# A head's query, gate and forget products in one row of groups, squares held back, and the last output weights loaded in another order

## The chip, the cores and the metric

The kernel runs on one core of one Trainium2 chip. The metric is the device time of one execution in microseconds (us). The kernel before takes 2017.0 us, the median of 3 runs (2017.0 to 2017.1).

## What is computed

The input is one sequence of 512 tokens of width 1024. A first block mixes tokens in two ways side by side, an HGRN2 recurrence with 4 heads of 128 and an NSA attention with 8 query heads of 64 in 2 groups, and adds a gated feed-forward step. Then come two layers of a second kind (L0 and L1), each with stick-breaking attention, differential attention and a feed-forward step of width 4096, and a last norm. All is in float32. The parts that the change touches are these:

```python
def hgrn2_mixer(hq, hf, hi, hg, lb, o_gain):
    q = jax.nn.silu(hq).reshape(B, T, H, dk)
    f = lb + (1.0 - lb) * jax.nn.sigmoid(hf)
    logf = jnp.log(f).reshape(B, T, H, dk)
    k = (1.0 - f).reshape(B, T, H, dk)
    ...
    o = rms_norm(o, o_gain) * jax.nn.silu(hg).reshape(B, T, H, dv)

def first_block(...):
    h = rms_norm(x, norm_mix[l])
    ...
    q = rms_norm(q.reshape(B, T, H, dh), q_norm[l])
    kc = rms_norm(compress(kc_raw, ...), k_norm[l, 0])
    vc = compress(vc_raw, ...)
    ...
    mix = jnp.concatenate([o_nsa, o_hgrn], axis=-1)
    x = x + mix @ w_out[l]

def differential_attention(q, k, v, lam):        # in L0 and L1
    ...
    p = jax.nn.softmax(jnp.where(allowed, s, neg), axis=-1)
    attn = p[:, :, 0] - lam * p[:, :, 1]
    return jnp.einsum('bhqk,bhkd->bhqd', attn, vh)
```

## The kernel before

Activations lie feature by token: a tile has 128 features on its partitions and all 512 tokens in its columns. A weight product ("group") takes a tile of 128 output features and goes over 8 tiles of input. `load_w` (L393 to L396) fetches a weight, ScalarE casts it into a high part (`_h`) and VectorE subtracts to get the low part (`_l`); `mm3` (L401, L402, L403) then does three matmuls for each input tile. There are two buffers for the parts and two PSUM banks of the kind "mm" for the results. `gemm_fm` runs such groups and calls an `emit` function on each finished bank; `gemm_nat` does the same with tokens on the partitions.

In the first block four streams of work (the HGRN heads, the set-up of NSA, its attention and the weight groups, `dense1`) are merged by `_drive`. A planner, `Clock`, keeps a rough time for each engine; a stream that would wait is passed over and the next one asked. The weight groups come in the order of a string, `ORDER1`: q1 is the query and forget product of head 1 (`whqf`), g0 is the output gate of head 0 (`whg`), n4 is the fifth NSA product (`wns`), i1 is the value product, v0 the NSA value and gate product (`wvsw`), w1 the second half of the output product (`wout1`); m4 waits for a head to be finished. The Tile scheduler then sets the final order on each engine.

The names that the steps below use:

- `emit_hgrn` (L607) and `emit_gate` (L627): scale a bank by the norm, take a sigmoid on ScalarE, multiply; for the forget product also a logarithm and a scan along the tokens. [...]
- `hgrn_head`: for each of the levels 64 to 1, decayed queries and keys (`qr`, `ke`) and 8 small matmuls `hpl` (L695), whose result VectorE selects into `at` (L697); then `hpd`, `hpo`, `hpv` (L754) and the head's output `ho`, transposed on TensorE (`ho_t`, L558).
- `emit_nsa` (L776): of each query product the parts `nq` and a square `nsq` (L789, ScalarE), and right behind it four matmuls `pq` (L792) that sum the square over a head's features. The groups after it follow in program order.
- `cs` (L927), `sc` (L930 to L948), `cpt` (L957): the scores of the compressed keys, their softmax on VectorE and ScalarE, and their transpose.
- the attention in 32 steps: scores `s` (L981 to L983), softmax `p`, transposes `pt` (L1014) and values `po`. The first matmul of a value (L1028) uses 32 rows and 64 columns of the array, the others (L1033) 128 rows and 64 columns.
- `gemm_late`: the other half of the output product, `wout0` (L0wo1 and L1wo1 in the layers). It starts when the attention has sent off its last scores, keeps four groups open until the last input exists, finishes them, and then runs the other four (`wout0x`, `L0wo1x`), whose weights come through the same two buffers.
- in L0 and L1 the scores `ds` (L1298 to L1301), transposes `dpt` (L1325) and values `dfo` (L1337) of the differential attention; `head_squares` (L532, `dsq`) reads the values' bank on ScalarE after each of its four steps. `L0wo` and `L1wo` are the output products, `add_residual` (L491) adds a bank to `X`.

## Time and profile before

| | before |
|---|---|
| median of 3 runs | 2017.0 us |
| profiled execution, its own time | 2017.01 us |
| span of that execution | 2015.1 us |
| TensorE busy | 1974.8 us, 98% of the span |
| VectorE busy | 1176.9 us, 58% |
| ScalarE busy | 885.1 us, 44% |
| mean granted clock of TensorE | 0.993 of full speed |

The span is what the profile covers; 1.9 us of the execution's own time lie around it. "Busy" is the share of the span in which an engine had an instruction running. The granted clock is given as a share of full speed, 1.00 for 2.4 GHz and 0.50 for 1.2 GHz.

### The profile page before, as it was taken

To read this page: it belongs to the slowest core of one execution; us is meant where nothing else is said; L and a number is where in the kernel's file an instruction comes from. 1 tells how busy PE (TensorE), PEld (TensorE's weight loads), DVE (VectorE), ACT (ScalarE), POOL (GpSimd) and SP (SyncE) were. 2 spreads that over 40 slices of the span, in tenths; PEclk is the share of its full clock that TensorE was granted. 3 is DMA by queue.
4 is the path that set the end of the run, shared out by engine and by line. 5 is a ranking of instruction groups with operands and counts; after the bars stand their busy time and mean duration, and the time that the engine had idled before them with its cause. 6 is when DMAs were issued, how large, how long until landed. Compare 5 with 4: busy or idle time off the path is not lost.

```text
span 2015.1 us, 25957 instructions
## 1 busy us (share of the span) xinstructions
PE 1974.8 (98%) x10197; PEld 1610.1 (80%) x10197; DVE 1176.9 (58%) x2032; ACT 885.1 (44%) x1497; POOL 45.2 (2%) x87
## 2 busy tenths in 40 slices
PE   8999999999999999999999999999999999999998
PEld 7888866788888878787778888888888778888887
DVE  7687676744444456557764444447466874444446
ACT  6645355522222235687542223335587743322223
POOL 1000000000000000001000000000000000000000
PEclk9999899999999999999999999999999999999999
DMA  6212100122222222212122222223221222222222
GB/s 206 67 60 88 51 22 22 53 95 96 99 97 95 95 89 92 82 40 84 61 84 98 100 95 94 94 94 105 79 64 58 63 76 98 98 94 94 95 94 74
DMA packets 50922, 168.65 MB, mean 84 GB/s; under 512 B 5808, under 2 KB 8240, under 8 KB 50800
## 3 DMA queue, kind: packets, MB, share of 16 engines
q1 hardware_dynamic: 47680, 161.93, 23.4%
q0 software_dynamic: 2976, 4.98, 1.2%
q8 instruction: 81, 1.33, 0.3%
q14 instruction: 41, 0.34, 0.1%
q10 hardware_dynamic: 144, 0.07, 0.0%
HBM read 160.14 MB, written 2.10 MB: 81 GB/s over the span
## 4 chain that ended last, share of the span: by engine, by line
PE 88%; DVE 5%; ACT 5%; issue 2%; DMA 1%; SPq 0%; DVEq 0%; POOL 0%; ACTq 0%
PE L0wf_p L403 6%; PE L0wf_p L401 6%; PE L0wf_p L402 6%; PE L1wf_p L403 5%; PE L1wf_p L401 5%; PE L1wf_p L402 5%; PE wgu_p L403 4%; PE wgu_p L401 4%; PE wgu_p L402 4%; PE wdn_p L401 2%; PE wdn_p L402 2%; PE wdn_p L403 2%; PE po L1033 1%; PE hpl L695 1%; PE pt L1014 1%
## 5 line engine op out<-in xcount | busy, mean ns | idle before, releaser
L395 ACT CAST L0wf_h<-L0wf_r 128x1024 fp32r<-128x1024 f32 x64 | 67.3, 1051 | 228.1 <-PE L0wf_p L403 224.8
L395 ACT CAST L1wf_h<-L1wf_r 128x1024 fp32r<-128x1024 f32 x60 | 63.1, 1051 | 219.7 <-PE L1wf_p L403 216.7
L403 PE MATMUL wgu_p<-h_l,wgu_h 128*128 128x512 f32 x328 | 128.8, 393 | 0.0
L401 PE MATMUL wgu_p<-h_h,wgu_h 128*128 128x512 f32 x328 | 128.7, 392 | 0.0
L402 PE MATMUL wgu_p<-h_h,wgu_l 128*128 128x512 f32 x328 | 128.6, 392 | 0.0
L395 ACT CAST wgu_h<-wgu_r 128x1024 fp32r<-128x1024 f32 x44 | 46.2, 1050 | 162.9 <-issue 62.8
L401 PE MATMUL L0wf_p<-L0u_h,L0wf_h 128*128 128x512 f32 x256 | 100.7, 393 | 0.0
L402 PE MATMUL L0wf_p<-L0u_h,L0wf_l 128*128 128x512 f32 x256 | 100.4, 392 | 0.0
L403 PE MATMUL L0wf_p<-L0u_l,L0wf_h 128*128 128x512 f32 x256 | 99.4, 393 | 0.0
L403 PE MATMUL L0wf_p<-L0m_l,L0wf_h 128*128 128x512 f32 x240 | 94.2, 393 | 0.0
L403 PE MATMUL L1wf_p<-L1m_l,L1wf_h 128*128 128x512 f32 x240 | 94.2, 393 | 0.0
L401 PE MATMUL L0wf_p<-L0m_h,L0wf_h 128*128 128x512 f32 x240 | 94.2, 392 | 0.0
L401 PE MATMUL L1wf_p<-L1m_h,L1wf_h 128*128 128x512 f32 x240 | 94.2, 392 | 0.0
L402 PE MATMUL L1wf_p<-L1m_h,L1wf_l 128*128 128x512 f32 x240 | 94.1, 392 | 0.0
L402 PE MATMUL L0wf_p<-L0m_h,L0wf_l 128*128 128x512 f32 x240 | 94.1, 392 | 0.0
L396 DVE TENSOR_TENSOR L0wf_l<-L0wf_r,L0wf_h 128x1024 fp32r<-128x1024 f32 x64 | 78.4, 1226 | 24.7 <-ACT L0wf_h L395 24.7
L401 PE MATMUL L1wf_p<-L1u_h,L1wf_h 128*128 128x512 f32 x224 | 88.1, 393 | 0.0
L402 PE MATMUL L1wf_p<-L1u_h,L1wf_l 128*128 128x512 f32 x224 | 87.9, 392 | 0.0
L396 DVE TENSOR_TENSOR L1wf_l<-L1wf_r,L1wf_h 128x1024 fp32r<-128x1024 f32 x60 | 73.5, 1225 | 23.2 <-ACT L1wf_h L395 23.2
L403 PE MATMUL L1wf_p<-L1u_l,L1wf_h 128*128 128x512 f32 x224 | 86.9, 393 | 0.0
L491 DVE TENSOR_TENSOR X<-X,L0wf_p 128x512 f32<-128x512 f32 x64 | 44.0, 687 | 67.1 <-PE L0wf_p L403 67.1
L491 DVE TENSOR_TENSOR X<-X,L1wf_p 128x512 f32<-128x512 f32 x56 | 38.6, 689 | 66.5 <-PE L1wf_p L403 66.5
(879 smaller groups left out, 5397.2 us busy)
## 6 DMA issues: line engine op xcount, KB each, us to landing
L0wf_r<-w_ff SPq DMA_DIRECT2D x64, 512.0 KB, 3.2
L1wf_r<-w_ff SPq DMA_DIRECT2D x60, 512.0 KB, 3.3
wgu_r<-w_gu SPq DMA_DIRECT2D x44, 512.0 KB, 3.2
wdn_r<-w_dn SPq DMA_DIRECT2D x22, 512.0 KB, 3.2
wns_r<-w_nsa SPq DMA_DIRECT2D x8, 512.0 KB, 3.5
L0wsb_r<-w_sbqk SPq DMA_DIRECT2D x8, 512.0 KB, 3.2
L0wdf_r<-w_dfqk SPq DMA_DIRECT2D x8, 512.0 KB, 3.2
L1wsb_r<-w_sbqk SPq DMA_DIRECT2D x8, 512.0 KB, 3.2
```

What stands on the lines that cost most here:

```text
L395: S.copy(hi[:, c], raw[:, c])
L396: V.tensor_tensor(lo[:, c], raw[:, c], _f(hi)[:, c], ALU.subtract)
L401: TE.matmul(ps, lh, rh, start=start, stop=False)
L402: TE.matmul(ps, ll, rh, start=False, stop=False)
L403: TE.matmul(ps, lh, rl, start=False, stop=stop)
L491: V.tensor_tensor(X[m], X[m], ps, ALU.add)
L695: TE.matmul(pl[:, b * 64 : (b + 1) * 64], ke[:, b * P : (b + 1) * P], qr[:, b * 64 : (b + 1) * 64], start=True, stop=True)
L1014: TE.transpose(pt[:, o + j * P : o + (j + 1) * P], p[g][:, j * P : (j + 1) * P], ident)
L1033: TE.matmul(po[g * 64 : (g + 1) * 64, 0:P], vsw[:, j, br * 128 + g * 64 : br * 128 + (g + 1) * 64], p[g][:, j * P : (j + 1) * P], start=Fa ...
```

## The change

`ORDER1` gets a new kind of entry. `x1` is the function `together`: it runs the query product of head 1, the output gate of head 0 and the forget product of head 1 in a row, without the sigmoids between them, and writes all sigmoids behind. `x2` does so for head 2 and gate 1, `x3` for head 3 and gate 2. The entries q1 to q3 and g0 to g2 are gone.

The sums of squares leave `emit_nsa`. A stream of its own, `nsa_squares`, sends off the four `pq` matmuls when the planner has the square done and a bank free; at the latest the next finished group does it (`catch_up`). `nsa_setup` waits for all six.

`gemm_late` loads its first two weights at its start and no longer waits for the last scores; its first two open groups use the "mm" banks, the other two the spare ones. Its third weight is loaded before the end, into buffers that are free by then ("kh", "kl").

The first value matmul of a step uses all 128 rows: `vz` holds the compressed values in four blocks of 128 columns, zero outside a block's own 32 rows. GpSimd makes it with a memset and four copies.

In the layers the planner has a value step wait until it believes that the last reader of the bank is done (`clock.read`).

```diff
-ORDER1 = "i0 q1 g0 n4 i1 q2 n6 g1 n0 m4 n7 n1 g2 m5 q3 n5 n2 n3 v0 g3 m7 w1"
+ORDER1 = "i0 x1 n4 i1 x2 n6 n0 m4 n7 n1 m5 x3 n5 n2 n3 v0 g3 m7 w1"

+    def read(self, tile):
+        self.take()
+        e, at = self.used.get(tile.tensor.name, ("PE", 0.0))
+        while e != "PE" and self.free["PE"] < at + 0.2:
+            yield None

-    def gemm_late(src, hs, emit, name, banks):
+    def gemm_late(src, hs, emit, name, scored, spare_banks):
         yield from until(lambda: all(x is not None for x in hs[:3]))
+        loaded = [load_w(src[b], f"{name}_{b}") for b in range(2)]
         for b in range(2):
-            wh, wl = load_w(src[b], f"{name}_{b}")
+            wh, wl = loaded[b]
+            if b == 1:
+                yield from until(scored)
+                loaded = [load_w(src[2], f"{name}_2", ("kh", "kl"))]
+                banks = spare_banks()
             for m in range(cols // P):
-                ps = banks.pop(0)() if banks else bank("mm", f"{name}_p{b}_{m}")
+                ps = bank("mm", f"{name}_p{b}_{m}") if b == 0 else banks[m]
...
-        yield from gemm_fm(src[2:], hs, emit, name + "x", 2 * (cols // P))
+        yield from gemm_fm(src[2:], hs, emit, name + "x", 2 * (cols // P), loaded=loaded)

+        def together(h, gates):
+            pre = []
+            def emit(m, ps):
+                catch_up()
+                x = sb("evt", f"x{h}_{len(pre)}")
+                V.tensor_tensor(x, ps, rb1, ALU.mult)
+                pre.append(x)
...
+            yield from gemm_fm(d["w_hqf"][2 * h : 2 * h + 1], h1, emit, f"whq{h}")
+            for g in gates:
+                yield from gemm_fm(d["w_hg"][g : g + 1], h1, emit, f"whg{g}")
+            yield from gemm_fm(d["w_hqf"][2 * h + 1 : 2 * h + 2], h1, emit, f"whf{h}")
+            x, hs_ = pre[-1], slice(h, h + 1)
+            forget = gated("kD", f"hk{h}", x)
+            q_ = gated("kC", f"hq{h}", pre[0])
+            gate = [gated("hs", f"hs{g}", pre[1 + i]) for i, g in enumerate(gates)]
+            with exp_ln_tables():
+                S.activation(x, forget, AF.Ln, scale=oml[:, hs_], bias=lbg[:, hs_])
...
+        def nsa_squares():
+            while len(squared) < 6:
+                yield from until(lambda: waiting or len(squared) == 6)
...
+                for w in (ready(sq), bank_free("t", 2)):
+                    for _ in w:
+                        if not waiting or waiting[0][0] != m:
+                            break
+                        yield None
+                if waiting and waiting[0][0] == m:
+                    add_squares()
+                    yield "low"

         def emit_nsa(m, ps):
+            catch_up()
...
             S.activation(sq, ps, AF.Square)
-            pq = bank("t", f"pq{m}")
-            for tb in range(NB):
-                TE.matmul(pq[:, 2 * tb : 2 * tb + 2], sq[:, tb * P : (tb + 1) * P], blk2, start=True, stop=True)
...
+            waiting.append((m, sq))

-                        TE.matmul(po[g * 64 : (g + 1) * 64, 0:P], comp["v"][32 * i : 32 * i + 32, g * 64 : (g + 1) * 64],
-                                  pct[g][32 * i : 32 * i + 32, qs], start=True, stop=False, tile_position=(32 * i, g * 64))
+                        TE.matmul(po[g * 64 : (g + 1) * 64, 0:P], vz[:, i * P + g * 64 : i * P + (g + 1) * 64],
+                                  pct[g][:, qs], start=True, stop=False)

-                     lambda n: both(ready(st[n], dv[NB - 1]), bank_free("o", 1) if n % NB == 0 else ()))))
+                     lambda n: both(ready(st[n], dv[NB - 1]), bank_free("o", 1) if n % NB == 0 else clock.read(st["do"])))))
```

The next pieces show TensorE's order at three places. Rows with x4 or x2 stand for as many instructions alike.

The first place is the levels of head 3, where the squares of the fourth query product (`nsq3`) are summed. Before:

```order
L695 MATMUL hpl3_8_1894<-qr3_8_1887,ke3_8_1888 128x64 x4
L403 MATMUL wvsw_p0_1982<-wvsw_1_l_1978,h1_6_h_145 128x280
L401 MATMUL wvsw_p0_1982<-wvsw_1_h_1977,h1_7_h_149 128x280
L402 MATMUL wvsw_p0_1982<-wvsw_1_h_1977,h1_7_l_150 128x280
L403 MATMUL wvsw_p0_1982<-wvsw_1_l_1978,h1_7_h_149 128x280
L792 MATMUL pq3_1951<-packed_82,nsq3_1949 128x2
L695 MATMUL hpl3_4_1932<-qr3_4_1913,ke3_4_1914 128x64 x4
L792 MATMUL pq3_1951<-packed_82,nsq3_1949 128x2 x3
L401 MATMUL wvsw_p1_2037<-wvsw_0_h_1971,h1_0_h_121 128x280
```

After:

```order
L411 MATMUL wvsw_p0_1941<-wvsw_1_l_1937,h1_6_h_145 128x280
L409 MATMUL wvsw_p0_1941<-wvsw_1_h_1936,h1_7_h_149 128x280
L410 MATMUL wvsw_p0_1941<-wvsw_1_h_1936,h1_7_l_150 128x280
L411 MATMUL wvsw_p0_1941<-wvsw_1_l_1937,h1_7_h_149 128x280
L747 MATMUL hpl3_4_2032<-qr3_4_1974,ke3_4_1975 128x64 x4
L409 MATMUL wvsw_p1_2005<-wvsw_0_h_1930,h1_0_h_121 128x280
L410 MATMUL wvsw_p1_2005<-wvsw_0_h_1930,h1_0_l_122 128x280
L411 MATMUL wvsw_p1_2005<-wvsw_0_l_1931,h1_0_h_121 128x280
L835 MATMUL pq3_1954<-packed_82,nsq3_1914 128x2 x4
L409 MATMUL wvsw_p1_2005<-wvsw_0_h_1930,h1_1_h_125 128x280
```

The four `pq3` were split by a level and followed the last of `wvsw_p0`; now they stand together, one level and three matmuls of `wvsw_p1` later, and the level `hpl3_8` stands 24 matmuls of `wvsw_p0` ahead of `hpl3_4`.

The second place is the start of the attention, around the transpose of the last head's output (`ho3_t`). Before, with the eight `cpt` matmuls in two rows right ahead of `s2_1`, that is four rows above this piece:

```order
L981 MATMUL s3_0_2428<-nk1h_2108,nq0_1175 128x256
L982 MATMUL s3_0_2428<-nk1l_2109,nq0_1175 128x256
L983 LDWEIGHTS masks_106
L983 MATMUL s3_0_2428<-masks_106 128x128
L981 MATMUL s3_1_2433<-nk1h_2108,nq0_1175 128x256
L982 MATMUL s3_1_2433<-nk1l_2109,nq0_1175 128x256
L983 LDWEIGHTS masks_106
L983 MATMUL s3_1_2433<-masks_106 128x128
L981 MATMUL s4_0_2462<-nk0h_2087,nq0_1175 128x384
L982 MATMUL s4_0_2462<-nk0l_2088,nq0_1175 128x384
L558 MATMUL ho3_t_2318<-packed_82,ho3_2303 128x128 x4
L1014 MATMUL pt0_0_2348<-packed_82,p0_2341 128x128 x2
```

After:

```order
L1061 MATMUL s3_0_2433<-nk1h_2114,nq0_1169 128x256
L1062 MATMUL s3_0_2433<-nk1l_2115,nq0_1169 128x256
L1063 LDWEIGHTS masks_106
L1063 MATMUL s3_0_2433<-masks_106 128x128
L572 MATMUL ho3_t_2296<-packed_82,ho3_2269 128x128 x4
L1094 MATMUL pt0_0_2332<-packed_82,p0_2325 128x128 x2
L1061 MATMUL s3_1_2438<-nk1h_2114,nq0_1169 128x256
L1062 MATMUL s3_1_2438<-nk1l_2115,nq0_1169 128x256
L1063 LDWEIGHTS masks_106
L1063 MATMUL s3_1_2438<-masks_106 128x128
L1037 MATMUL cpt0_2376<-packed_82,sc_2149 128x128 x3
L409 MATMUL wout1_p0_0_2342<-ho3_m_h_2301,wout1_0_h_2337 128x512
```

The transposes `cpt0` and `cpt1` moved from ahead of `ho3_t` to behind it, and the last score product `s4_0` ahead of it is gone. Further up, all twelve last matmuls of `whg3` stood behind the last `cs` before; they all stand ahead of it now.

The third place is the end of the differential attention in L0 (L1 is alike). Before:

```order
L402 MATMUL L0wo1_p1_0_8638<-L0do3_m_h_8625,L0wo1_1_l_8634 128x512
L403 MATMUL L0wo1_p1_0_8638<-L0do3_m_l_8626,L0wo1_1_h_8633 128x512
L401 MATMUL L0wo1_p1_1_8648<-L0do3_m_h_8625,L0wo1_1_h_8633 128x512
L401 MATMUL L0wl_8578<-L0do3_m_h_8625,L0wo1_0_h_8580 128x512
L402 MATMUL L0wl_8578<-L0do3_m_h_8625,L0wo1_0_l_8581 128x512
L403 MATMUL L0wl_8578<-L0do3_m_l_8626,L0wo1_0_h_8580 128x512
L402 MATMUL L0wo1_p1_1_8648<-L0do3_m_h_8625,L0wo1_1_l_8634 128x512
L403 MATMUL L0wo1_p1_1_8648<-L0do3_m_l_8626,L0wo1_1_h_8633 128x512
L401 MATMUL L0wo1x_p0_0_8680<-L0do0_m_h_7900,L0wo1x_0_h_8675 128x512
L401 MATMUL L0wo1x_p0_1_8694<-L0do0_m_h_7900,L0wo1x_0_h_8675 128x512
```

After:

```order
L409 MATMUL L0wo1_p0_0_8576<-L0do3_m_h_8642,L0wo1_0_h_8565 128x512
L410 MATMUL L0wo1_p0_0_8576<-L0do3_m_h_8642,L0wo1_0_l_8566 128x512
L409 MATMUL L0wo1_p0_1_8597<-L0do3_m_h_8642,L0wo1_0_h_8565 128x512
L410 MATMUL L0wo1_p0_1_8597<-L0do3_m_h_8642,L0wo1_0_l_8566 128x512
L411 MATMUL L0wo1_p0_0_8576<-L0do3_m_l_8643,L0wo1_0_h_8565 128x512
L411 MATMUL L0wo1_p0_1_8597<-L0do3_m_l_8643,L0wo1_0_h_8565 128x512
L409 MATMUL L0wl_8633<-L0do3_m_h_8642,L0wo1_1_h_8571 128x512
L410 MATMUL L0wl_8633<-L0do3_m_h_8642,L0wo1_1_l_8572 128x512
L411 MATMUL L0wl_8633<-L0do3_m_l_8643,L0wo1_1_h_8571 128x512
L409 MATMUL L0wo1x_p0_0_8677<-L0do0_m_h_7917,L0wo1_2kh_8628 128x512
```

The groups that were finished first were those of the spare bank (`L0wl`); now they are those of the "mm" banks, and the group behind them, `L0wo1x_p0_0`, reads the weight `L0wo1_2kh`, whose cast stands some twenty instructions further up on ScalarE than that of `L0wo1x_0_h` did.

## Rows read from the trace of the kernel before

**Rows 1.** The page: busy time, share of the span and instructions of each engine.

```profile
PE 1974.8 (98%) x10197; PEld 1610.1 (80%) x10197; DVE 1176.9 (58%) x2032; ACT 885.1 (44%) x1497; POOL 45.2 (2%) x87
```

**Rows 2.** TensorE's waits: line, what it waited for, us in total, times, longest.

```profile
PE pq L792 <- ACT nsq L789: 4.5, 4, 2.2
PE s L981 <- ACT p L993: 2.2, 2, 1.6
...
PE L0dfo L1337 <- ACT L0dsq L532: 1.2, 2, 0.9
...
PE L0wo1x_p L401 <- ACT L0wo1x_h L395: 0.8, 1, 0.8
...
PE cpt L957 <- DVE sc L948: 0.8, 1, 0.8
PE hpl L695 <- DVE ck_u L834: 0.7, 1, 0.7
...
PE L0wo1x_p L402 <- DVE L0wo1x_l L396: 0.6, 1, 0.6
...
PE wout0x_p L402 <- DVE wout0x_l L396: 0.6, 1, 0.6
PE pkc L853 <- DVE ck_u L837: 0.6, 1, 0.6
```

**Rows 3.** Windows: stretch, length, busy PE, PEld, DVE, ACT, POOL, PEclk, DMA share, GB/s.

```profile
200.76:204.17 3.41, 3.41 (x17) 3.41 (x16) 2.56 (x4) 1.85 (x3) 0.00 (x0) 0.50 0.33 126
...
207.59:214.40 6.81, 6.34 (x29) 6.35 (x30) 2.25 (x6) 0.83 (x2) 0.00 (x0) 0.50 0.01 1
214.40:221.24 6.84, 6.84 (x32) 6.84 (x32) 3.59 (x15) 0.35 (x1) 0.00 (x0) 0.50 0.01 2
...
1013.13:1016.55 3.42, 3.42 (x9) 2.65 (x8) 2.76 (x4) 2.34 (x5) 0.00 (x0) 0.50 0.75 220
```

**Rows 4.** Timeline of the levels of head 3: start, us, instruction, idle before.

```profile
196.68 1.00 PE L695 MATMUL hpl<-qr,ke 128*128 128x64 f32 x8
...
199.15 1.05 PE L792 MATMUL pq<-packed,nsq 128*128 128x2 f32 x8 [1.47 <-ACT nsq L789]
...
208.06 0.59 PE L792 MATMUL pq<-packed,nsq 128*128 128x2 f32 x2 [2.23 <-ACT nsq L789]
...
213.03 1.80 PE L695 MATMUL hpl<-qr,ke 128*128 128x64 f32 x8
```

**Rows 5.** Window from the last compressed score to `ho3_t`, columns as above.

```profile
240.08:256.63 16.55, 14.23 (x84) 11.53 (x84) 15.22 (x49) 10.71 (x27) 0.00 (x0) 1.00 0.09 32
```

**Rows 6.** Window of the matmuls of `whg3` alone: PE, PEld, DVE, PEclk.

```profile
240.08:242.77 2.69, 2.69 (x12) 1.99 (x11) 0.00 (x0) 1.00 0.00 0
```

**Rows 7.** Timeline from the last compressed score to the first values.

```profile
244.34 1.28 ACT L631 ACT_TABLE_LOAD   x1
245.63 0.63 ACT L631 ACTIVATE gsg<-gx 128x512 f32<-128x512 f32 x1
...
252.31 1.09 PE L957 MATMUL cpt<-packed,sc 128*128 128x128 f32 x8 [0.76 <-DVE sc L948]
...
255.52 0.69 DVE L551 TENSOR_TENSOR ho<-hpv,ho_rn 128x512 f32<-128x512 f32 x1
255.63 0.38 PE L981 MATMUL s<-nk1h,nq 128*128 128x256 f32 x1 [1.56 <-ACT p L993]
...
261.80 0.43 PE L1028 MATMUL po<-cpt,vcn 32*64 32x128 f32 x4
...
262.17 0.66 PE L1033 MATMUL po<-p,vsw 128*64 128x128 f32 x8
```

**Rows 8.** Timeline at three waits of L0.

```profile
955.29 0.71 PE L1337 MATMUL L0dfo<-L0dv,L0dp 128*128 128x128 f32 x4 [0.30 <-ACT L0dsq L532]
...
974.82 0.50 PE L401 MATMUL L0wo_p<-L0mix_h,L0wo_h 128*128 128x512 f32 x1 [1.29 <-DVE X L491]
...
1004.30 0.69 ACT L561 ACTIVATE L0do_m_h<-L0do_t,L0sg 128x512 fp32r<-128x512 f32 x1 [2.32 <-PE L0do_t L558]
```

More of the change, by code (lines that the diff above doesn't have):

```diff
@@ L633, in emit_gate, with gated @@
             V.tensor_tensor(t, x, sg, ALU.mult)
+        def together(h, gates):
+            pre = []
+            def emit(m, ps):
+                catch_up()
+                x = sb("evt", f"x{h}_{len(pre)}")
+                V.tensor_tensor(x, ps, rb1, ALU.mult)
+                pre.append(x)
+            def gated(tag, name, x):
+                t = sb(tag, name)
+                S.activation(t, x, AF.Sigmoid)
+                return t
+            yield from gemm_fm(d["w_hqf"][2 * h : 2 * h + 1], h1, emit, f"whq{h}")
[8 more added lines that the diff above has]
+                S.activation(x, forget, AF.Ln, scale=oml[:, hs_], bias=lbg[:, hs_])
+            c = sb("kE", f"hc{h}")
+            V.tensor_tensor_scan(c, chunk_reset, x, 0.0, ALU.mult, ALU.add)
+            V.tensor_scalar(forget, forget, noml[:, hs_], oml[:, hs_], ALU.mult, ALU.add)
+            V.tensor_tensor(q_, pre[0], q_, ALU.mult)
+            for i, g in enumerate(gates):
+                V.tensor_tensor(gate[i], pre[1 + i], gate[i], ALU.mult)
+                hs[g] = gate[i]
+            hk[h], hc[h], hq[h] = forget, c, q_
+            yield True
         def hgrn_head(h):
@@ L774, in block1, with add_squares, catch_up @@
         comp = {}
+        waiting, squared = [], []
+        def add_squares():
+            m, sq = waiting.pop(0)
+            pq = bank("t", f"pq{m}")
+            for tb in range(NB):
+                TE.matmul(pq[:, 2 * tb : 2 * tb + 2], sq[:, tb * P : (tb + 1) * P], blk2, start=True, stop=True)
+            if m < 4:
+                V.tensor_copy(qss[:, 0:32].rearrange("p (b i g) -> p b i g", b=NB, i=4)[:, :, m, :],
+                              pq[:, 0:8].rearrange("p (b g) -> p b g", g=2))
+            else:
+                V.tensor_copy(qss[:, 32 + 8 * (m - 4) : 40 + 8 * (m - 4)], pq[:, 0:8])
+            squared.append(m)
+        def catch_up():
+            while waiting:
+                add_squares()
+        def nsa_squares():
+            while len(squared) < 6:
+                yield from until(lambda: waiting or len(squared) == 6)
+                if not waiting:
+                    return
+                m, sq = waiting[0]
+                for w in (ready(sq), bank_free("t", 2)):
[4 more added lines that the diff above has]
+                if waiting and waiting[0][0] == m:
+                    add_squares()
+                    yield "low"
         def emit_nsa(m, ps):
+            catch_up()
             if m >= 4:
@@ L885, in nsa_setup @@
             yield True
-            yield from until(lambda: 1 in kraw, lambda: nq[3] is not None)
+            yield from until(lambda: len(squared) == 6)
             rr = small("rr", [P, NB])
@@ L1043, in values @@
                 return 0.25 * (b + 1)
-            yield from until(lambda: len(nk) == 2, lambda: "gates" in comp, lambda: "linear" in comp)
+            yield from until(lambda: len(nk) == 2, lambda: "gates" in comp, lambda: "linear" in comp, lambda: "v" in comp)
+            vz = sb("hs", "vz")
+            G.memset(vz, 0.0)
+            for i in range(4):
+                r = slice(32 * i, 32 * i + 32)
+                G.tensor_copy(vz[r, i * P : (i + 1) * P], comp["v"][r])
             yield from pipeline(len(units), 2, (
@@ L1053, in dense1 @@
         def dense1():
-            def hqf(h):
-                return gemm_fm(d["w_hqf"][2 * h : 2 * h + 2], h1, emit_hgrn, f"whqf{h}", 2 * h)
             def hg(h):
@@ L1083, in dense1 @@
                     yield from nsa(n, n + 1)
-                elif k == "q":
-                    yield from hqf(n)
+                elif k == "x":
+                    yield from together(n, ((), (0,), (1,), (2,))[n])
                 elif k == "g":
@@ L1095, in dense1 @@
                     yield from gemm_fm(d["w_out"][n], mix[4 * n : 4 * n + 4], add_residual, f"wout{n}")
-            yield from until(lambda: "scored" in comp)
-            yield from gemm_late(d["w_out"][0], Late(mix, 0), add_residual, "wout0",
-                                 [lambda: bank("s", "wl0"), lambda: bank("s", "wl1")])
+            yield from gemm_late(d["w_out"][0], Late(mix, 0), add_residual, "wout0", lambda: "scored" in comp,
+                                 lambda: [bank("s", f"wl{i}") for i in range(2)])
         run(gemm_fm(d["w_hqf"][0:2], h1, emit_hgrn, "whqf0", 0, spare(2, "sph")))
-        _drive(clock, hgrn_all(), nsa_setup(), nsa_attention(), dense1())
+        _drive(clock, nsa_squares(), hgrn_all(), nsa_setup(), nsa_attention(), dense1())
         h2 = normed(C["norm_ffn"], "h2_")
```

20 lines of the change are left out of this document (8 added, 12 removed).

## The prediction

> **What bounds the kernel now.** I began with the engine totals. TensorE is busy for 1974.8 of 2015.1 us [rows 1], so the time is its matmuls plus about 40 us in which it does nothing. A change of order can win two things: the waits, and time in which the same matmuls run slowly. The list of TensorE's waits comes next [rows 2]. Its largest entry is `pq`, the sums of squares, which waits 4.5 us in four places for ScalarE's square; the rest is 0.6 to 2.2 us each. Then the windows by granted clock [rows 3]: in three neighbouring stretches around the levels of head 3 TensorE was granted 0.50, that is 1.2 GHz, and was busy for 3.41 + 6.34 + 6.84 = 16.59 us; a fourth stretch, of 3.42 us, lies at the end of L0's attention. The timeline shows what stood in front of them [rows 4]: a wait of 1.47 us for `nsq2`, then half clock; a wait of 2.23 us for `nsq3`, then half clock again. So `pq` costs more than its own 4.5 us.
>
> **The change, part by part.** The sum is made against the profiled execution's own 2017.01 us (span 2015.1 and 1.9 around it), which is the median of the runs, 2017.0.
>
> *Squares: the two large waits.* They are 1.47 + 2.23 = 3.70 us [rows 4]. The order now puts `pq2` between matmuls of `wns3` and `pq3` behind 24 matmuls of `wvsw_p0`, a level and three matmuls more, so the squares have cover and both waits go. Next is late what feeds the levels: `hpl3_4` then waits for its exponential and multiply (I estimate 0.6 us), `wvsw_p1` for its low part (0.2), `nkpb` for the chain of small VectorE steps behind `pq3` (0.7). That is 1.5 us, bounded by none and by the 3.70 won. Gain 2.2.
>
> *Squares: the clock.* A level at full clock takes 1.00 us, at half clock 1.80 [rows 4], so 16.59 us at half clock would shrink by 16.59 x (1 - 1.00/1.80) = 7.4 us. At most it is half, 8.3; at least nothing, if the clock falls there anyway. I take 7.0, since at full speed VectorE's selects stand closer behind each level. What could drop it again is the new waits of 0.6 and 0.7, which are shorter than the two that stood ahead of the half clock.
>
> *Query, gate and forget in a row.* In the earlier heads the waits of `hpl` (0.7) and `pkc` (0.6) for the compressed keys and about half of the remaining 0.8 of `pq` lie under matmuls that moved ahead of them [rows 2]: 1.7. The forget gates of heads 1 and 2 come 5 to 6 us later than before, and with them logarithm, scan and levels; I count four new waits of some 0.2 us, 0.9 in all. A table load takes 1.28 us [rows 7], and the order of ScalarE has 26 of them instead of 24, because the scheduler spreads the sigmoids again: only in x2 do two share a load. If both extra loads lay on the path, that would be 2.56. Bounds of the new waits: 0 and 2.6. Gain 0.8.
>
> A load's price in the trace is the 1.28 us and nothing more, since the sigmoid starts 1.29 us after the load does [rows 7]. The Trainium skill, page "ScalarE: Activation LUTs", section "What ACT_TABLE_LOAD costs", adds a drain and gives about 2.66 us for each change of set; by that, two loads would cost 5.3 us instead of 2.56. This trace does not show the drain, so the row decides.
>
> *The start of the attention.* Here the change takes cover away. Before, 16.55 us pass between the last `cs` and `ho3_t`, and TensorE has work for 14.23 of them [rows 5]; VectorE is busy for 15.22, so its chain of softmax steps (`sc`, `cs`, then `ho`) sets the length, and TensorE's idle 2.32 us are the waits at `cpt` and `s` [rows 7]. In the changed order the twelve matmuls of `whg3` in it, 2.69 us [rows 6], stand ahead of the last `cs`, the eight `cpt`, 1.09 us [rows 7], behind `ho3_t`, and one score product of some 0.6 with them: 4.4 us of work leave the stretch. VectorE's chain is the same but for the end: `hpv3` is done some 4 us earlier, so `ho` need not come as far behind `sc`, and I take 1.2 us off. So TensorE waits 4.4 - 1.2 = 3.2 us more, some 5.5 in all and most of it in one piece before `ho3_t`. The moved matmuls do other work's covering elsewhere, which is in the terms above. Bounds: 0, if they are worth as much where they are now, and 4.4. Loss 3.2.
>
> That piece is longer than any wait that stood ahead of a half clock. A wait of 1.47 us was enough at one place [rows 4] and one of 1.56 was not at another [rows 7]. I take one stretch like that of L0, 3.42 us [rows 3], at half speed: 1.7 lost. Bounds: 0, and two such stretches, 3.4.
>
> The Trainium skill, page "TensorE: Matmul & The Clock Gate", section "HAM oscillation", says that waiting between bursts of matmuls takes TensorE to half rate, and the next burst starts slowly. The trace agrees at `pq` and not at `s`, where the clock stayed at 1.00. By the page alone the loss of 1.7 stands.
>
> *First value matmul with 128 rows.* Four alone start 0.37 us ahead of the next form, while four more of the same form add 0.66 - 0.43 = 0.23 [rows 7]; so a change of the tile's shape costs some 0.15 us. In the new order there are six changes fewer. Gain 0.7 (bounds 0 and 0.9). GpSimd's memset and copies of `vz` are off the path: their input is ready before head 3's levels and the engine is idle there.
>
> *Late weights.* In the first block `wout0x` waits 0.6 for its low part [rows 2]; the third weight is now there before. Gain 0.6. In each layer `L0wo1x` waits 0.8 + 0.6 [rows 2] for a weight whose buffer came free too late; now it is loaded early. What is late next is the last input: only two matmuls stand between `L0do3_t` and the first that reads `L0do_m_h`, whose copy takes 0.69 us [rows 8], so I count a new wait of 0.5. Gain 0.9 a layer, 1.8. The half clock behind it in L0, 3.42 us [rows 3], goes with the wait: 1.7 (0 at least).
>
> *The planner's order in the layers.* `L0wo` waits 1.29 for an addition to `X` that stands behind a maximum of 1.2 us on VectorE [rows 8]. In the new order the addition to that bank stands several matmuls ahead of its next use; I count 1.2 a layer, 2.4 (bounds 0 and 2.6). Of the waits of `L0dfo` for `L0dsq`, 1.2 a layer [rows 2], the 0.30 [rows 8] gets eight score matmuls for cover; the 0.9 gets one matmul more, 0.2. So 0.5 a layer, 1.0.
>
> **Sum.** 2.2 + 7.0 + 0.8 - 3.2 - 1.7 + 0.7 + 0.6 + 1.8 + 1.7 + 2.4 + 1.0 = 13.3, so 2017.0 - 13.3 = 2003.7 us.
>
> **The rivals.**
>
> 1. *The half clock at head 3 has another cause.* From 214.40 to 221.24 TensorE was busy without a gap and still at 0.50 [rows 3], among levels of small matmuls that stay where they are. If they hold the clock down, the 7.0 is missing: 2010.7 us. Against it: the levels before 200 us ran at full clock, as the 1.00 at 196.68 shows [rows 4].
>
> 2. *It doesn't do what it says.* The sigmoids are not together (26 table loads), ScalarE is late at heads 1 to 3, and both loads land on the path: 2.56 more, 2006.3 us. For it: levels wait for exponentials behind those loads. Against: ScalarE is busy only 44% [rows 1].
>
> 3. *Better.* The moved groups cover as much as before, the clock stays up at `ho3_t`, and the new waits at head 3 are only half as long: 1.7 + 1.6 + 0.8 more, 1999.6 us.
>
> 4. *Most of it is given back.* Rival 1 and, at `ho3_t`, a full loss of 4.4 and two slow stretches: 13.3 - 7.0 - 1.2 - 1.7 = 3.4, so 2013.6 us, no difference that can be told (below).
>
> 5. *Slower.* The long wait before `ho3_t` drops the clock, and the attention that follows, with its matmuls of 64 to 128 columns between switches of shape, does not bring it back. Each us at half clock costs 0.44. The other terms leave 13.3 + 1.7 = 15.0 to eat, so it decides from 34 us at half clock on; with 60 us of the attention it would be 2017.0 - 15.0 + 26.6 = 2028.6 us. Against it: before, the longest such stretch was 13.65 us and ended by itself [rows 3].
>
> **How the numbers follow.** The forecast, 2003.7, gets 0.46; rival 1 0.14, rival 2 0.10, rival 3 0.14, rival 4 0.10, rival 5 0.06. A measurement of this kernel tells about 0.2%, 4 us, from no change, so faster is below 2013.0: forecast and rivals 1 to 3, 0.84. Rival 4 is the same, 0.10, and rival 5 slower, 0.06. The range leaves out rivals 4 and 5 and the far end of rival 3: 1998 to 2013.
>
> **What would show it.** Right: no wait of `pq` above 0.2 us; 1.00 as granted clock from 197 to 222 us; a wait of 4 us or so before `ho3_t` with a short stretch at 0.50 behind it; no wait of `L0wo1x` and `L0wo` in the list, a wait of about 0.5 us of `L0wo1` for `L0do_m_h`. Wrong: 0.50 in the levels of head 3 without a wait ahead; a wait before `ho3_t` below 3 us (then VectorE's chain got shorter than I think) or several slow stretches in the attention; new waits above 1 us at the levels of heads 1 to 3 behind a table load.

## The result and the profile after

The changed kernel takes 2000.6 us (median of 4 runs, 1998.8 to 2001.0) against 2017.0 before. The ratio is 0.9928 with a 95% interval of 0.9908 to 0.9947: faster by 0.7%, 3.1 us below the forecast of 2003.7 and inside its range. Single runs of one kernel lie apart, and the mean granted clock goes with their time: in the experiments' comparisons, the kernel before took 2009.0 to 2010.9 us in the 7 runs with a mean clock of 0.996 or 0.997 and 2011.7 to 2018.2 us in the 26 with 0.991 to 0.995. The four runs of the changed kernel all have 0.997 or 0.998. Against the median of those 7 runs, 2009.5, it gains 8.9 us; so some 7 of the 16 us between the medians go with a lower clock, which not every run of the kernel before has.

The profiled run after took 2001.03 us, 16.0 less than the one before, and its span is 15.9 shorter. TensorE's busy time and the entries of its list of waits that matter, first the page, then the list (us in total, times, longest):

```profile
PE 1966.0 (98%) x10197; PEld 1604.9 (80%) x10197; DVE 1174.8 (59%) x2032; ACT 887.2 (44%) x1499; POOL 48.7 (2%) x92
```

```profile
PE ho_t L572 <- DVE ho L565: 3.9, 1, 3.9
...
PE s L1061 <- ACT p L1073: 1.7, 4, 0.9
...
PE pq L835 <- ACT nsq L877: 1.5, 2, 1.3
...
PE hpl L747 <- DVE ke L741: 0.7, 2, 0.4
...
PE L0dfo L1419 <- ACT L0dsq L546: 0.6, 1, 0.6
...
PE L0wo_p L409 <- ACT L0do_m_h L575: 0.3, 1, 0.3
```

Against [rows 1], 8.8 us of the 15.9 are busy time and 7.1 are waits. Against [rows 2], the two large waits of `pq`, those of `wout0x`, `L0wo1x` and the one of 1.29 us of `L0wo` for `X` [rows 8] are gone. New are 3.9 us before the transpose of the last head's output (`ho_t`) and 1.3 us at `pq`, where the first query's square (`nsq0`) is summed (`pq0`). The windows of after (columns as in [rows 3]) show the clock:

```profile
126.37:129.78 3.41, 3.41 (x16) 3.12 (x15) 2.62 (x9) 2.69 (x8) 0.00 (x0) 0.50 0.00 0
197.00:222.00 25.00, 24.56 (x204) 23.33 (x205) 19.45 (x47) 11.67 (x19) 5.84 (x11) 1.00 0.26 64
...
245.84:249.25 3.41, 3.21 (x14) 2.80 (x15) 2.96 (x11) 2.06 (x6) 0.00 (x0) 0.50 0.00 0
```

```profile
232.02:246.04 14.02, 9.27 (x57) 7.59 (x56) 12.94 (x42) 6.48 (x20) 0.00 (x0) 0.99 0.11 37
```

The levels of head 3, at 0.50 for 16.59 us of busy time before [rows 3], run at 1.00. L0's stretch is gone. Two of 3.41 us are new: one at 126 us, one at 246. The last window goes from the last `cs` to `ho3_t` and answers to [rows 5]: it is 2.5 us shorter, and 5.0 us of TensorE's work have left it.

The new wait ahead of the stretch at 126 us is that of the first query's square. Timeline of TensorE, VectorE and ScalarE ahead of it:

```profile
118.97 1.00 DVE L898 TENSOR_TENSOR ck_b<-nraw,packed 64x496 f32<-64x496 f32 x1
...
120.01 1.23 DVE L404 TENSOR_TENSOR wns_l<-wns_r,wns_h 128x1024 fp32r<-128x1024 f32 x1
...
121.27 0.69 DVE L444 TENSOR_TENSOR nq<-wns_p,nq 64x512 fp32r<-64x512 f32 x1
...
121.99 0.58 ACT L443 CAST nq<-wns_p 64x512 fp32r<-64x512 f32 x1 [3.09 <-DVE nq L444]
...
123.82 0.69 DVE L444 TENSOR_TENSOR nq<-wns_p,nq 64x512 fp32r<-64x512 f32 x1
124.55 0.60 ACT L877 ACTIVATE nsq<-wns_p 128x512 f32<-128x512 f32 x1 [1.98 <-DVE nq L444]
...
125.19 1.05 PE L835 MATMUL pq<-packed,nsq 128*128 128x2 f32 x8 [1.29 <-ACT nsq L877]
```

Read it from the bottom: `pq` waits for the square; the square waits 1.98 us for VectorE's second subtraction of the query's split (`nq`), and ScalarE's second copy had waited 3.09 us for the first one. That one stood behind a product for the compressed keys (`ck_b`) and a weight's low part (`wns_l`).

### The profile page after: what moved, and what is told of

It reads as the page before. It is cut to its first block, busy times and chain, and to the rows that moved or that the text cites. A ratio compares the mean times of both kernels' runs of the same rounds, so it can differ in the third digit from the quotient of the medians.

```text
span 1999.2 us, 25966 instructions
## 1 busy us (share of the span) xinstructions
PE 1966.0 (98%) x10197; PEld 1604.9 (80%) x10197; DVE 1174.8 (59%) x2032; ACT 887.2 (44%) x1499; POOL 48.7 (2%) x92
## 4 chain that ended last, share of the span: by engine, by line
PE 89%; ACT 5%; DVE 4%; issue 2%; DMA 1%; SPq 0%; POOL 0%; DVEq 0%; ACTq 0%
PE L0wf_p L411 6%; PE L0wf_p L409 6%; PE L0wf_p L410 6%; PE L1wf_p L409 5%; PE L1wf_p L411 5%; PE L1wf_p L410 5%; PE wgu_p L409 4%; PE wgu_p L411 4%; PE wgu_p L410 4%; PE wdn_p L409 2%; PE wdn_p L410 2%; PE wdn_p L411 2%; PE po L1113 1%; PE hpl L747 1%; PE pt L1094 1%
```

## The experiments

Where nothing else is said, an experiment starts from the changed kernel, and a distance is one of medians. The ratio given with each is its time over that of the kernel before, which ran beside it, with a 95% interval. There were three such comparisons, in which the kernel before took 2015.8, 2016.2 and 2015.9 us; the 2000.6 us of the changed kernel come from the comparison of the result, with 2017.0 for the kernel before. So a distance from it of 1 us or so may be one of comparisons. The theory at the start: held squares moved `pq` off the path at head 3, and the row of query, gate and forget gate moved the cover away from `ho3_t`.

### Squares sent off at once

```diff
             waiting.append((m, sq))
+            catch_up()
```

> The changed kernel with one edit undone: each sum of squares is sent off right behind its square again, as before; order of groups, late weights and the rest stay as changed. Theory (the held squares bring the two waits and, through them, the clock): the waits of pq come back, 3 us or more in all, a stretch of 10 us or more at 0.50 comes back at the levels of head 3, and the time rises by about 2.2 + 7.0 us, from 2000.6 to about 2010. Rival (the clock at head 3 depends on the order of the groups around the levels, not on the waits of pq): the waits come back but no long stretch at 0.50, and the time is about 2003.

Measured: 1994.2 us (1993.7 to 1997.3), ratio 0.9904 [0.9888, 0.9920]. That is 6.4 us *faster* than the changed kernel; the theory fell, and so did the rival. (No run of the two overlaps, 1997.3 at most against 1998.8 at least; the intervals of the ratios do, from 0.9908 to 0.9920.) Its waits and its window from the last `cs` to `ho3_t`:

```profile
PE pkc L934 <- DVE ck_u L918: 1.4, 1, 1.4
...
PE ho_t L572 <- DVE ho L565: 1.1, 1, 1.1
PE ho_t L572 <- ACT p L1074: 0.9, 1, 0.9
```

```profile
224.18:240.98 16.80, 15.91 (x94) 13.61 (x94) 16.08 (x38) 10.21 (x23) 0.00 (x0) 1.00 0.30 94
```

The 1.1 us are at the transpose of head 1, the 0.9 us at that of head 3. There is no wait of `pq` at head 3, though nothing is held: the new order of the products alone gives the squares their cover. And in the window TensorE has work for 15.91 us instead of 9.27, because the last `cs` now comes 7.8 us earlier (224.18 against 232.02), so 24 matmuls of `whg3` stand behind it, where the changed kernel has none. The only half clock ahead of the final norm is 3.41 us at the very start.

### The old order of query and gate, squares held

```diff
-    ORDER1 = "i0 x1 n4 i1 x2 n6 n0 m4 n7 n1 m5 x3 n5 n2 n3 v0 g3 m7 w1"
+    ORDER1 = "i0 q1 g0 n4 i1 q2 n6 g1 n0 m4 n7 n1 g2 m5 q3 n5 n2 n3 v0 g3 m7 w1"
```

(`q` runs the query and the forget product of a head again, each with its own sigmoid, as before.)

> The changed kernel with the old order of groups: query, gate and forget products apart, each with its own sigmoid, in the places of before; held squares, late weights and the rest stay as changed. Theory (the new order takes cover away at the start of the attention): the wait of 3.9 us before the last head's transpose shrinks to below 2.5, the stretch at 0.50 behind it goes, and the time falls by about 3 us, to about 1997 to 1998. Rival A (the new order covers the early heads): waits of 2 us or more come back in the first 190 us, and the time is about 2003. Rival B (the wait before the transpose comes from the scores of the compressed keys being ready earlier, which the held squares do): it stays at 3 to 4 us, and the time is within 1 us of 2000.6.

Measured: 1999.2 us (1998.8 to 2000.6), ratio 0.9926 [0.9911, 0.9942]: 1.4 us below the changed kernel, and the intervals overlap. Its waits:

```profile
PE ho_t L572 <- DVE ho L565: 4.2, 2, 3.9
...
PE pq L835 <- ACT nsq L877: 1.1, 2, 0.8
```

The 3.9 us before `ho3_t` stay with the old order, as rival B has it. With the run above, where they go: it is the held squares, not the row of products, that take the cover away.

### Both undone

Both edits above together; late weights, value matmul and layers stay as changed.

> The changed kernel with both the old order of query and gate groups and the squares' sums sent off at once; the late weights, the 128-row value matmul and the layers stay as changed. It completes the square of order and squares, beside the changed kernel (2000.6), sums at once alone (1994.2) and old order alone (1999.2). Theory A, either part alone moves the two squares off the path and neither is needed beside the other: with both undone the waits of pq at head 3 come back (3.7 us in two places) and with them 0.50 of clock in the levels, some 15 to 17 us of it: 2010 to 2013 us. Theory B, the waits of pq go through something else in the change (the late weights or the planner of the layers also move what stands before them): no pq wait above 0.5 us and 1994 to 2001 us.

Measured: 2005.4 us (1999.3 to 2007.2), ratio 0.9950 [0.9932, 0.9967]. The waits are those of before, the half clock is not:

```profile
PE pq L835 <- ACT nsq L877: 4.5, 4, 2.2
```

```profile
198.87:202.28 3.41, 3.41 (x16) 3.41 (x16) 2.70 (x6) 1.57 (x3) 0.00 (x0) 0.50 0.45 156
...
209.11:212.52 3.41, 3.41 (x17) 3.41 (x17) 0.84 (x3) 0.00 (x0) 0.00 (x0) 0.50 0.01 2
```

The waits of 1.47 and 2.23 us are back to the hundredth [rows 4], and up to the first value matmul TensorE's order is that of the kernel before. Still only 6.8 us follow at half clock, where the profiled run of before has stretches of 3.41 and 13.65 us [rows 3]; theory A's time, 2010 to 2013 us, was missed with them. The profiled run took 2001.2 us at a mean clock of 0.996, one more took 1999.3 at 0.997, and the other four lie at 2004.3 to 2007.2 with 0.994 or 0.995. As 0.002 of 2004 us is 4 us, most of the distance between the two groups is more time at half clock; where it lies is not shown, as only one run has a trace.

The square of order and squares is now: old and at once 2005.4, new and at once 1994.2, old and held 1999.2, new and held 2000.6. The new order alone removes the two waits, and holding alone leaves 0.8 us of them. Together they save no more than holding does, and 6.4 us less than the new order does.

### Which held squares cost it

```diff
             waiting.append((m, sq))
+            if m >= 4:
+                catch_up()
```

> The changed kernel, but the sums of the two squares of the keys (m 4 and 5) are sent off at once, and those of the four queries stay held. In its order pq0 stands where it stood, the first cs moves up from row 856 to 817 of TensorE, and the two cpt stand ahead of ho3_t. Theory A, holding costs at two places, the wait of 1.3 us at pq0 with the half clock behind it, and the late cs with the wait of 3.9 us before ho3_t and its half clock: the first stays (1.2 to 1.4 us at pq0, 0.50 near 126 us), the wait before ho3_t falls below 2 us: 1996 to 1998 us. Theory B, it is the held query squares alone that set the place of cs: the wait before ho3_t stays above 3 us, 2000 us.

The counterpart has `m < 4`:

> The counterpart: the sums of the four queries' squares are sent off at once and those of the two keys stay held. In its order pq0 stands two matmuls earlier among others, cs starts at row 802, and the cpt stand ahead of ho3_t. Theory A, holding costs at pq0 and before ho3_t: both are gone, no wait above 0.5 us at pq0, none above 2 us before ho3_t, no 0.50 near 126 us: 1994 to 1996 us. Theory B, the held key squares cost as much by delaying kcT and with it cs: wait before ho3_t above 3 us and 1999 to 2001 us.

Measured: the keys' sums at once 1996.7 us (1995.2 to 1997.8), ratio 0.9912 [0.9895, 0.9928]; the queries' at once 2004.7 (2003.1 to 2006.3), 0.9951 [0.9937, 0.9965]. In the first, as theory A has it, `pq0` still waits 1.27 us with half clock behind it and the wait before `ho3_t` is gone. In its place are the two waits of the kernel before, of `s` and of `cpt` (0.8 us), and 3.41 us at half clock follow them too:

```profile
PE s L1063 <- ACT p L1075: 2.2, 2, 1.6
...
PE pq L835 <- ACT nsq L877: 1.7, 3, 1.3
```

```profile
126.73:130.14 3.41, 3.41 (x15) 3.12 (x15) 2.46 (x9) 2.45 (x8) 0.00 (x0) 0.50 0.00 0
...
246.20:249.61 3.41, 3.41 (x18) 2.03 (x17) 2.53 (x6) 1.86 (x6) 0.00 (x0) 0.50 0.02 5
```

The second has neither of the two either, and is 8 us slower all the same, which both theories miss. Its list has these instead:

```profile
PE s L1063 <- ACT p L1075: 3.0, 5, 1.5
PE pt L1096 <- DVE p L1080: 2.3, 3, 1.4
...
PE pkc L935 <- DVE ck_u L919: 1.4, 1, 1.4
...
PE hpl L747 <- DVE ke L741: 1.1, 2, 0.9
PE ho_t L572 <- DVE ho L565: 1.1, 1, 1.1
```

By the times at which each stage begins in the two traces, counted from head 0's transpose, the second kernel gains 3.5 us up to head 1's transpose, where the first one waits at `pq0` and runs at half clock. It gives 2.3 back up to head 2's transpose (`pkc`), loses 2.5 from there to the last `cs` (among them a wait of `hpl` of 0.9 us and a half-clock stretch from 208.52 to 211.94 us, worth some 1.5), 1.3 up to `ho3_t`, and 3.9 between the first and the last value matmul, of which 1.4 are one wait of `pt`. So the place of a few sums in the order changes the planner's choices down to the end of the attention, and no single wait is the price of holding.

### The first square's place

In the kernel with the keys' sums at once, the first query's square is issued ahead of its split:

```diff
+            sq = sb("evt", f"nsq{m}")
+            if m == 0:
+                S.activation(sq, ps, AF.Square)
             if m < 4:
                 nq[m] = stacked_q(ps, f"nq{m}")
...
-            sq = sb("evt", f"nsq{m}")
-            S.activation(sq, ps, AF.Square)
+            if m > 0:
+                S.activation(sq, ps, AF.Square)
```

> The kernel with the keys' sums at once (1996.7 us), and the square of the first query, nsq0, issued on ScalarE ahead of the query's split instead of behind it. Theory A, the wait of 1.27 us at pq0 is one of queue order: nsq0 stands behind the second copy of the split, which waits for VectorE's subtraction, and that stands behind the products for the compressed keys; ahead of the split it can run some 6 us earlier, the wait goes, and the half clock behind it, 3.41 us, too: 1993 to 1994.5 us, best of all so far. Theory B, the matmuls before pq0 are what lowers the clock there or pq0, which moves 16 rows up, waits as long at its new place: 1996 to 1997.5 us, with 0.50 near 126 us.

Measured: 1994.7 us (1993.2 to 1996.0), ratio 0.9897 [0.9881, 0.9913]; 2.0 below its base, which ran in another comparison; the intervals overlap, and so do the runs, so the rows decide.

```profile
119.25 0.59 ACT L874 ACTIVATE nsq<-wns_p 128x512 f32<-128x512 f32 x1
...
120.38 0.95 PE L835 MATMUL pq<-packed,nsq 128*128 128x2 f32 x8
```

```profile
119.00:130.00 11.00, 10.71 (x66) 8.97 (x66) 10.74 (x24) 4.72 (x14) 0.00 (x0) 1.00 0.16 48
```

The square runs over 5 us earlier than in the changed kernel (119.25 against 124.55), `pq` does not wait, and the clock stays up: the wait was one of queue order on ScalarE, as theory A says. That the half clock goes with the wait is likely: of the six traces with this wait (1.26 to 1.29 us at `pq0`) five have half clock right behind it, of the seven without it none. Theory A's figure, "1993 to 1994.5", was 0.2 too low at its upper end.

The other way at the same wait was to send off the first query's and the keys' sums at once (`m in (0, 4, 5)`):

> Sums at once for the first query and the two keys; those of queries 1 to 3 held. TensorE's order from the levels of head 3 on is the one of the kernel with the keys' sums at once (1996.7 us), but pq0 stands two rows further up among other matmuls and pkcs 53 rows later. Theory A, the held first square is what cost the 1.27 us and the half clock behind it: both gone, but the waits of 1.05 us before ho1_t and 1.35 us before pkc, seen with all sums at once, come in their place: 1995 to 1997 us, no 0.50 near 126 us. Theory B, they come with 0.50 behind them: 1997 to 1999 us.

Measured: 2001.1 us (1998.9 to 2003.2), ratio 0.9931 [0.9915, 0.9946]; slower than either theory. As theory A has it, the wait at `pq0` and the half clock behind it are gone. The predicted waits before `ho1_t` (1.1) and `pkc` (1.4) came without half clock behind them, but a third, of `wvsw_p`, has it:

```profile
PE wvsw_p L409 <- DVE gl L884: 1.0, 1, 1.0
```

```profile
206.88:213.70 6.82, 6.82 (x32) 6.82 (x33) 3.34 (x16) 0.47 (x1) 0.00 (x0) 0.50 0.01 2
```

### Small matmuls without a wait

The loop of the compressed scores yields at its usual rank instead of a low one, so its 64 matmuls of 32 columns stand in a row:

```diff
-                        yield "low"
+                        yield True
```

> The changed kernel with one edit more: the sixteen pieces of the compressed keys' scores are sent off one after the other instead of letting six or twelve matmuls of the weight groups in between, so that the last gate product and half a value product stand behind them. Theory (the wait before the last head's transpose is VectorE's chain without matmuls beside it): the wait of 3.9 us falls below 1, the stretch at 0.50 behind it goes, and the time falls by 4 to 6 us, to about 1995 to 1996.5. Rival (the wait moves elsewhere, since the matmuls that now cover this place leave another uncovered): the transposes of the compressed scores or the first values wait 3 us or more, and the time stays at 1999 to 2001.

Measured: 2003.5 us (2001.7 to 2008.3), ratio 0.9951 [0.9933, 0.9970]. The wait before `ho3_t` falls from 3.88 to 1.61 us, and the kernel is 2.9 us slower, which neither the theory nor the rival has:

```profile
217.69 9.71 PE L1007 MATMUL cs<-kcT,nq 128*128 128x32 f32 x64
```

```profile
217.69:222.06 4.37, 4.37 (x42) 4.37 (x41) 2.51 (x6) 0.22 (x1) 2.29 (x5) 1.00 0.66 149
222.06:227.40 5.34, 5.34 (x27) 5.34 (x27) 0.21 (x2) 0.00 (x0) 0.00 (x0) 0.50 0.17 65
```

TensorE is busy without a gap through both windows and falls to half clock in the middle of the row; it stays there up to 232.30 us. The last wait ahead of the row is one of 0.43 us, at 203.00. All six runs have a lower mean clock, 0.990 to 0.995, than those of the changed kernel. So a wait is not needed for it, and rival 1 of the prediction, that small matmuls hold the clock down, names something that exists.

### The late weights, the planner's entry, the value matmul

Each is undone alone. First the late weights, with the old order of the first finished groups:

```diff
-                loaded = [load_w(src[2], f"{name}_2", ("kh", "kl"))]
...
-            yield from gemm_fm(src[2:], hs, emit, name + "x", 2 * (cols // P), loaded=loaded)
+            yield from gemm_fm(src[2:], hs, emit, name + "x", 2 * (cols // P))
```

> The changed kernel with the old last output product: it starts after the last scores, its first open groups use the spare banks, and the third weight is loaded into the same two buffers. Theory (the late weights alone brought these): waits of 0.8 and 0.6 us come back in each layer and 0.8 us in the first block, with them the stretch at 0.50 at the end of the first layer's attention; in all about 1.4 + 1.6 + 1.6 + 1.7 = 6.3 us, so about 2007. Rival (most of the layers' gain is the planner's other order of the values): the time is about 2003.

Measured: 2005.4 us (2003.1 to 2008.1), ratio 0.9956 [0.9938, 0.9973], 4.8 more. That median lies between two groups, three runs at 2003.1 to 2003.3 with a mean clock of 0.997 or 0.998, and three at 2007.5 to 2008.1 with 0.994; against the first, which have the changed kernel's clock, the part is worth 2.5 us. The waits come back (L1's are like L0's), 3.1 us in all:

```profile
PE L0wo1x_p L409 <- ACT L0wo1x_h L403: 0.7, 1, 0.7
...
PE wout0x_p L410 <- DVE wout0x_l L404: 0.6, 1, 0.6
...
PE L0wo1x_p L410 <- DVE L0wo1x_l L404: 0.5, 1, 0.5
```

L0's half clock does not come back in the profiled run, which is one of the three long ones. Its 1.7 us therefore can't be given to this part; the two stretches at 128 and 247 us are twice as long here (6.8 us each), in work that the edit leaves as it is.

Next, the planner's entry:

```diff
-                     lambda n: both(ready(st[n], dv[NB - 1]), bank_free("o", 1) if n % NB == 0 else clock.read(st["do"])))))
+                     lambda n: both(ready(st[n], dv[NB - 1]), bank_free("o", 1) if n % NB == 0 else ()))))
```

> The changed kernel without the one new entry in the planner's conditions of the layers' value units (the time at which the last state copy is read), which moves score matmuls ahead of the next L0dfo. The prediction counted it in the planner's 2.4 + 1.0 for both layers. Theory A: it is what puts eight score matmuls ahead of the L0dfo that waited 0.30 us, and the wait of L0wo for X is gone through the late weights' new order: a little slower, 2001 to 2002 us, with a wait of some 0.3 us of dfo back in each layer and none of wo for X. Theory B: it carries the whole gain of the planner's order: the waits of wo for X (1.2 us a layer) come back as well, 2003 to 2004 us. Theory C: it moves nothing that waits, 2000 to 2001 us.

Measured: 2004.5 us (2003.2 to 2006.0), ratio 0.9950 [0.9935, 0.9965], 3.9 more; theory B, and a little beyond it.

```profile
PE L0wo_p L409 <- DVE X L505: 1.3, 1, 1.3
PE L1wo_p L409 <- DVE X L505: 1.3, 1, 1.3
...
PE L0dfo L1419 <- ACT L0dsq L546: 1.1, 2, 0.8
```

One entry in one condition is the whole gain of the planner's order in both layers: the additions to `X` are late again, and the 0.6 of `L0dfo` is 1.1.

This run shows one thing more. Up to the first value matmul TensorE has the order of the changed kernel and the same waits, 1.29 us at `pq0` (125.39) and 0.43 us at a level of head 3 (201.45), but not the same clock:

```profile
126.57:129.98 3.41, 3.41 (x25) 3.00 (x25) 3.28 (x9) 3.13 (x9) 0.00 (x0) 1.00 0.00 0
203.83:207.24 3.41, 3.41 (x16) 3.41 (x16) 3.17 (x14) 0.42 (x1) 0.00 (x0) 0.50 0.01 2
```

Last, the value matmul:

```diff
-                        TE.matmul(po[g * 64 : (g + 1) * 64, 0:P], vz[:, i * P + g * 64 : i * P + (g + 1) * 64],
-                                  pct[g][:, qs], start=True, stop=False)
+                        TE.matmul(po[g * 64 : (g + 1) * 64, 0:P], comp["v"][32 * i : 32 * i + 32, g * 64 : (g + 1) * 64],
+                                  pct[g][32 * i : 32 * i + 32, qs], start=True, stop=False, tile_position=(32 * i, g * 64))
...
```

(GpSimd's memset and copies go with it.)

> The changed kernel with the first value matmul back on 32 rows instead of 128; TensorE's order is the same row by row. Theory A, each change of the tile's shape costs some 0.15 us and six of them come back: 0.7 us more (bounds 0 and 0.9), 2001.3 us, and the waits stay as they are. Theory B, the sum of what is left when old order and old squares (2005.4 us against 2016.2 before), the late weights (4.8 us) and the planner's entry (3.9 us) are taken out, 10.8 - 8.7 = 2.1 us, lies here: 2002.7 us.

Measured: 2002.8 us (2001.1 to 2003.0), ratio 0.9937 [0.9922, 0.9951], 2.1 more and next to the figure of theory B. From the first to the last value matmul, with the changed kernel's 128 rows and then with 32 rows:

```profile
251.54:362.98 111.44, 109.25 (x811) 76.99 (x810) 78.25 (x251) 56.87 (x158) 0.00 (x0) 1.00 0.07 25
```

```profile
252.25:364.79 112.54, 110.33 (x811) 76.74 (x810) 78.35 (x251) 56.77 (x158) 0.00 (x0) 1.00 0.07 25
```

The order is the same row by row, and the stretch is 1.1 us longer, all of it busy time. The other 1.0 of the medians has no place in the traces but the start, where this run lies 0.7 behind; its six runs have a mean clock of 0.995 to 0.998, so part of it may be half clock.

## Why the prediction was right

The size was right within 3.1 us, and the sums of the parts come near too, some of them by luck. Each part undone alone, in medians against the changed kernel:

| part | terms of the prediction | gain expected | measured |
|---|---|---|---|
| order of products and squares, with the start of the attention | 2.2 + 7.0 + 0.8 - 3.2 - 1.7 | 5.1 | 4.8 |
| late weights | 0.6 + 1.8 + 1.7 | 4.1 | 4.8 |
| planner's order in the layers | 2.4 + 1.0 | 3.4 | 3.9 |
| first value matmul | 0.7 | 0.7 | 2.1 |

They add up to 15.6, and 2016.2 - 2000.6 is 15.6 too, closer than the spread of the runs can promise. The first two entries are medians of six runs that fall into two groups by their clock: at the changed kernel's clock the late weights are worth 2.5 us and not 4.8, and order and squares together nothing that shows (1999.3 us at 0.997 against 2000.9 and 2001.0). Inside the parts:

*Squares, the waits: right, and a little small.* 3.70 us became one wait of 0.44 at a level of head 3, a gain of 3.3 instead of 2.2; the waits of `wvsw_p1` and `nkpb` did not come.

*Squares, the clock: right in the trace, uncertain in size.* Head 3 ran at 1.00 from 197 to 222 us. But 7.0 was sized from one run of before, and the 7 runs of before at a mean clock of 0.996 or 0.997 show that it can have much less. The kernel with both parts undone shows the same two waits with 6.8 us at half clock behind them, worth 6.8 x 0.44 = 3.0, and its profiled run is only 0.2 us above the changed kernel's, while the medians are 4.8 apart.

*What the change of squares is: wrong.* The prediction gave the gain at head 3 to the squares, without asking what the new order does by itself. The order alone removes both waits and the half clock at head 3 (1994.2 us), and holding the squares on top costs 6.4.

*Query, gate and forget in a row: 0.8 expected, about -0.4 measured.* From 88 to 186 us the waits went from 1.8 to 2.2. Those of `hpl` and `pkc` went as expected. The wait of 1.29 at `pq0` was not foreseen: I had looked at the squares of head 3 alone and not at where the first one stands in ScalarE's queue, and its half clock, 3.41 us or some 1.5, was in no term. With it one sign of the prediction, no wait of `pq` above 0.2 us, did not come. Nor is it the row's alone: with the same row and the sums at once, and with held squares and the old order, `pq0` does not wait so. Of the table loads (ACT_TABLE_LOAD) one stands ahead of a wait, 0.61 us of `hpv` for `hsq` at 176.48 (timeline of ScalarE):

```profile
174.25 1.28 ACT L709 ACT_TABLE_LOAD   x1
175.54 0.63 ACT L709 ACTIVATE qc<-hc 128x512 f32<-128x512 f32 x1
176.08 0.26 ACT L546 ACTIVATE hsq<-hpv 128x128 f32<-128x128 f32 x1
```

That it is one of the two extra loads is not shown; the bounds of 0 to 2.6 hold it.

*Start of the attention: right.* Expected were 3.2 us more of waits, most in one piece of about 4, and one stretch of 3.42 at half speed. Measured: 3.88 + 0.87 instead of 2.32 [rows 7], so 2.4 more, and 3.41 us at 0.50. The cover that left was 14.23 - 9.27 = 5.0 instead of 4.4, and VectorE's chain became 2.5 us shorter instead of 1.2. The prediction read the loss from the new order of TensorE and did not say which part of the change makes it; by the experiments it is the held squares. What `ho3_t` waits for in the end is VectorE again (timeline):

```profile
245.31 0.68 DVE L565 TENSOR_TENSOR ho<-hpv,ho_rn 128x512 f32<-128x512 f32 x1
```

*First value matmul: mis-sized.* 1.1 us in its own stretch, above the upper bound of 0.9. I had counted the changes of shape in the order and priced each from one place; which of the two was too low is open.

*Late weights and layers: right for the waits.* No wait of `L0wo1x` or of `L0wo` for `X` is left; `L0wo` waits 0.3 for `L0do_m_h`, where 0.5 was expected. L0's 1.7 stays open, as told above. Part of the 3.1 us between forecast and result lies where the change does nothing: up to the first product of head 1 (36.12 us before, 34.76 after) the profiled run after is 1.4 us ahead of the one before.

Rivals 1, 4 and 5 did not come in the changed kernel's profiled run: head 3 ran at full clock, and the clock recovered after each stretch. Rival 2 came only in that 0.61 us. Rival 1 is not excluded: without the planner's entry, head 3 had 3.41 us at 0.50 with no more than 0.43 us of wait ahead. Rival 3's time, 1999.6, is nearer than the forecast, but two of its three reasons failed: the moved groups did not cover as much, and the clock did fall at `ho3_t`. Two kernels of the study beat both given ones: the squares sent off at once, 1994.2 us, and the keys' sums at once with the first square ahead of its split, 1994.7.

## What to carry to other kernels

When a change has two parts for one wait, cost each alone before adding them: here the new order had already moved the squares off the path, and the second cure moved other work into the way. A wait on an engine's result is first a question of that engine's queue: moving one 0.6 us instruction ahead of two that wait removed a 1.27 us wait and, in the trace, the half clock behind it. And work that covers a chain of small steps on another engine was worth most here between the chain's start and its end: with 24 matmuls of `whg3` behind the last `cs` the waits in that window are 0.9 us, with all of them ahead of it 4.8. A last one for the measuring: compare the granted clock of every run before a difference of medians is given to a part of a change.

## What the hardware did unexpectedly

The same waits are not always followed by the same clock, even where TensorE runs the same instructions in the same order. The 1.29 us at `pq0` had 0.50 for 3.41 us behind them in the changed kernel, for 6.8 us with the old late weights, and the clock stayed at 1.00 without the planner's entry. 0.76 and 1.56 us at `cpt` and `s` had 1.00 behind them before [rows 7] and in three kernels of the study (both undone, the queries' sums at once, the first query's and the keys' sums at once), and 0.50 for 3.41 us in two others: the keys' sums at once, and that with the first square ahead:

```profile
243.80:247.21 3.41, 3.41 (x18) 2.33 (x18) 2.05 (x7) 2.10 (x6) 0.00 (x0) 0.50 0.02 5
```

The 3.9 us before `ho3_t` had half clock at their end, for 3.4 or 6.8 us, in all five traces that have this wait. And in the row of 64 matmuls of 32 columns, with no wait in the 14 us ahead of it and no gap in it, the clock came down as well. The Trainium skill, page "TensorE: Matmul & The Clock Gate", section "HAM oscillation", puts half rate down to the waits between bursts of matmuls. The 3.9 us before `ho3_t` agree with it; the row of 64 without a wait does not, and behind the waits of 1.3 to 1.6 us both clocks are found, so there the rows decide. What tells these cases apart was not found, and it is the largest part of what is uncertain in the sizes above.
